# Weight ring buffers of 4128 instead of 4096 bytes a partition in a two-layer attention trunk

## The chip, the cores and the metric

One core of a Trainium2 chip. The metric is the device time of one execution in microseconds; the kernel before takes 651.13 us, the median of three runs (650.99 to 651.28). It must return the reference's output.

## The reference, cut to what matters

x is 256 tokens of 1024 channels, all float32. Each of two layers does this:

```python
h = rms_norm(x, gain)
proj = einsum('bsd,de->bse', h, w_in)              # 1024 -> 9808 columns
(qa, ka, va, ga, qb, kb, vb, gb, qc, kc, vc, gc,
 q_idx, k_idx, w_idx, f_logit, merge_logit) = split(proj)
oa = moba_attention(rope(qa), rope(ka), va) * silu(ga)
ob = dsa_attention(rope(qb), rope(kb), vb, rope(q_idx), rope(k_idx), w_idx) * silu(gb)
oc = forgetting_attention(qc, kc, vc, log_sigmoid(f_logit + f_bias)) * silu(gc)
y = einsum('nbsw,nwd->bsnd', stack([oa, ob, oc]), w_branch)
merged = sum(sigmoid(merge_logit) * y, over n)
x = x + merged @ w_out
```

A last RMS norm follows. The weights (w_in, w_branch, w_out) are read once each, 104 MB in all, and every weight meets all 256 tokens.

## The kernel before, in words

**Precision.** TensorE works on the type float32r. To come near float32, each operand is held as two tiles, a high part (h) and the rest (l), and a product is three matmuls: high times high, low times high, high times low. The normalised and transposed input is hTh and hTl (eight slices of 128 channels by 256 tokens each); the gated branch outputs are og0h, og0l, og1h, og1l; V and, later, the merged sum are in v0 and v1.

**The weights' way.** A chunk of weights, up to 1 MB, comes by a DMA on SP's queue into one of three raw buffers (2048 columns). ScalarE writes the high part of a piece of it (1024 columns) into a buffer wh (L350), VectorE subtracts and writes the rest into wl (L354), both in `piece`. wh and wl are two rings of six buffers each (`R_RING = 6`). `piece` uses the first a * b columns of a buffer and nothing else.

**Units of TensorE.** A projection unit (`unit_b`) takes one pair wh, wl, and writes 128 output columns for all 256 tokens: sixteen matmuls with a slice of wh stationary, for each slice one with hTh and one with hTl moving, then eight with wl stationary and hTh moving, in groups of six (`mm_ops`, L395); a matmul is 128x128 by 256 columns. There are 64 such units in a layer, and one like them whose weights have 80 columns (kwf). A branch unit (`unit_y`) has twelve matmuls: for each of four slices wh with the branch's high and low part, then wl with the high part. There are 24 in a layer, and two of them share a pair wh, wl. In the units for V and for the output (`unit_a`, and `first_v` with L938) the ring buffer is the moving operand of 512 columns and hTh, hTl or V is the stationary one; a unit takes four pairs wh, wl and has 24 matmuls. The last two output units of the kernel are one of 512 columns split in two of 256.

**Between the units** stand the scores of a head pair (`scores`, L558 to L560), transposes of the probabilities (L648) and their product with V (L663 to L666), with VectorE and ScalarE doing the softmax, the rotary embedding, and the choice of keys (L772, L792, L793).

**Order.** `Plan` lists all operations with an estimated cost, a due time, what they read and write and which ring buffer they need, and simulates the engines: at each step it takes, for the engine that is free first, the ready operation with the lowest due time, and emits it. Costs come from functions of the number of columns (t_act, t_dve, t_mm and the like). The order of every engine, the DMAs' order and the turn of the ring buffers are fixed by that when the kernel is built.

**Addresses.** All tiles lie in one pool, each tile behind the one declared before it, in steps of 32 bytes a partition. Starts in a partition, modulo 256: hTh and hTl 192; v0, v1 and the og tiles 0; the block-diagonal keys bd 0; raw0 to raw2 192; wh0 to wh5 and wl0 to wl5 all 192, since 4096 is a multiple of 256; behind the rings q (qh, ql) 192, e 192, pth and ptl 64. A slice of hTh, og or bd lies a multiple of 512 bytes behind its tile's start, and so does a slice of a full weight piece; a slice of the 80-column piece is 320 bytes long, so that its slices start at 192, 0, 64, 128 and so on.

The lines that the change and the prediction touch:

```python
R_RING = 6
tag("raw", R_RAW, [128, 2048])
tag("wh", R_RING, [128, 1024], F32R)
tag("wl", R_RING, [128, 1024], F32R)
p[0].v = T(p[0])[:, :a * b].rearrange("p (a b) -> p a b", a=a)          # L349
ACT.activation(p[0].v, sel(c.v), AF.Copy)                               # L350
DVE.tensor_tensor(p[1].v, sel(c.v), p[0].v.bitcast(F32), op=ALU.subtract)   # L354
his = [(lambda k=k: p[0].v[:, k], lambda k=k, h=h: h[:, k], [p[0]] + hT_all[i])
       for k in range(KC) for i, h in enumerate((hTh, hTl))]            # L412
PE.matmul(o(), a(), b(), start=first and i == 0, stop=last and i == n - 1)  # L395
```

Of the kernel before, what the change touches and what calls it, by code (L numbers as in the profile page):

```python
# [10 lines left out]
F32R = mybir.dt.float32r  # L11
# [20 lines left out]

R_RING = 6
R_RAW = 3
LAG = {("ACT", "DVE"): 142.0, ("DVE", "ACT"): 128.0, ("DVE", "POOL"): 155.0, ("POOL", "ACT"): 75.0,
       ("ACT", "POOL"): 75.0, ("PE", "ACT"): 197.0, ("PE", "DVE"): 196.0, ("PE", "POOL"): 200.0,
       ("ACT", "PE"): 170.0, ("DVE", "PE"): 200.0, ("POOL", "PE"): 170.0,
# [61 lines left out]
class Plan:  # L99
# [37 lines left out]
    def run(self, slack):  # L137
# [4 lines left out]
        while ready:  # L142
            best = {}
            cand = []
            for o in ready:
# [15 lines left out]
                for w in o.ways:  # L161
                    e = w[0]
                    tt = max(t, free.get(e, 0.0))
                    for b in o.bufs:
                        if b.last is not None and b.last.eng != e:
                            tt = max(tt, b.last.end + LAG.get((b.last.eng, e), SEM))
                    for d in o.deps:
                        tt = max(tt, d.end + d.lag + LAG.get((d.eng, e), 0.0 if d.eng == e else SEM) + (0.0 if d.eng == e else o.margin))
                    if e == "POOL" or (e == "DVE" and o.port):
# [64 lines left out]
def hybrid_trunk(ctx, tc, x, norm_gain, w_in, forget_bias, w_branch, w_out, final_gain, consts, out):  # L234
# [9 lines left out]
    def tag(name, n, shape, dt=F32):  # L244
        plan.tag(name, [pool.tile(shape, dt, name=f"{name}{i}") for i in range(n)])
# [67 lines left out]
    k_acc = [Tok() for _ in range(KC)]  # L313

    tag("raw", R_RAW, [128, 2048])
    tag("wh", R_RING, [128, 1024], F32R)
    tag("wl", R_RING, [128, 1024], F32R)
    plan.tag("bd", bd)
    for nm, n, cols, dt in (("qh", 3, S, F32R), ("ql", 3, S, F32R), ("rsh", 2, S, F32), ("rr", 2, S, F32),
                            ("th", 2, S, F32), ("g", 4, S, F32), ("e", 4, 384, F32), ("st", 8, 8, F32),  # L320
# [737 lines left out]
```

## Time and profile before

| | |
|---|---|
| median of three runs | 651.13 us (650.99 to 651.28) |
| the profiled execution | 651.38 us, of which the span shown is 649.5 us |
| TensorE matmuls busy | 639.6 us, 4836 records |
| weight loads busy | 610.9 us |
| VectorE busy | 550.0 us |
| ScalarE busy | 398.8 us |
| DMA, mean | 163 GB/s, 105.56 MB |

The span is the time from the first to the last of the program's own instructions. A TensorE matmul is pipelined: its recorded duration (some 280 ns for 256 columns) is longer than the time from its start to the next one's start, which is what a stream of them costs. The timeline lists starts; a row "x4" stands for four like instructions in a row, and the next row's start is that of the matmul behind them. Times in the timeline have two decimals, so that an interval is best taken over many matmuls and divided.

### The profile page before, as it was taken

How to read it: one execution, taken by the hardware profiler on the slowest of the kernel's cores; microseconds unless marked ns; L12 is line 12 of the kernel's file. 1: busy time of each engine (PE TensorE's matmuls, PEld its weight loads, DVE VectorE, ACT ScalarE, POOL GpSimd, SP SyncE). 2: the span in 40 equal slices, each digit the busy share in tenths (PEclk: the TensorE clock that was granted, in tenths of full speed). 3: DMA queues.
4: the chain of work that ended last, by engine and by line, in shares of the span. 5: the costliest groups of instructions: out<-in, count | busy, mean ns of one | idle time of the engine just before them, and what ended most of it. 6: DMA issues, size and time to landing. Idle time of an engine off the chain costs nothing.

```text
span 649.5 us, 12568 instructions
## 1 busy us (share of the span) xinstructions
PE 639.6 (98%) x4836; PEld 610.9 (94%) x4836; DVE 550.0 (85%) x1334; ACT 398.8 (61%) x799; POOL 89.0 (14%) x96
## 2 busy tenths in 40 slices
PE   8999999999999999999999999999999999999996
PEld 7999999899998999999889999998999989999985
DVE  8899998876969889998488999878587888999873
ACT  6765575764756667575486646767466565747531
POOL 1324112000000222200005403020000003121000
PEclk9999999999999999999999999999999999999998
DMA  9747446455472553473455545634635354453611
GB/s 296 230 143 244 131 130 227 131 166 170 150 229 66 177 173 123 146 256 134 150 175 166 174 143 166 217 97 163 207 118 195 109 178 140 160 162 121 236 34 66
DMA packets 93854, 105.56 MB, mean 163 GB/s; under 512 B 4321, under 2 KB 82401, under 8 KB 93793
## 3 DMA queue, kind: packets, MB, share of 16 engines
q1 hardware_dynamic: 93504, 104.36, 48.7%
q8 instruction: 38, 0.62, 0.4%
q10 hardware_dynamic: 288, 0.39, 0.2%
q14 instruction: 24, 0.19, 0.1%
HBM read 103.69 MB, written 1.05 MB: 161 GB/s over the span
## 4 chain that ended last, share of the span: by engine, by line
PE 83%; DVE 12%; issue 2%; DMA 1%; ACT 1%; SPq 0%; POOL 0%; POOLq 0%; ACTq 0%
PE proj L395 72%; DVE wl L354 4%; PE t L648 2%; PE proj L938 1%; PE s L560 1%; PE s L558 1%; PE o L666 1%; PE s L559 1%; DVE e L621 1%; DMA x<-in_x_dram 1%; PE o L663 1%; DVE isc L793 1%; DVE isc L772 1%; DVE t L792 1%; DVE rsh L440 1%
## 5 line engine op out<-in xcount | busy, mean ns | idle before, releaser
L350 ACT ACTIVATE wh<-raw 128x1024 fp32r<-128x1024 f32 (+1 forms) x190 | 199.5, 1054 | 147.8 <-PE proj L395 125.8
L354 DVE TENSOR_TENSOR wl<-raw,wh 128x1024 fp32r<-128x1024 f32 (+1 forms) x190 | 238.7, 1265 | 41.0 <-ACT wh L350 36.5
L395 PE MATMUL proj<-hTh,wh 128*128 128x256 f32 (+1 forms) x1040 | 257.5, 284 | 0.1
L395 PE MATMUL proj<-hTl,wh 128*128 128x256 f32 (+1 forms) x1040 | 255.9, 283 | 0.0
L395 PEld LDWEIGHTS proj<-hTh,wh 128*128 128x128 f32 (+1 forms) x1040 | 198.2, 191 | 1.6 <-DVE bd1l L697 0.3
L395 PEld LDWEIGHTS proj<-hTl,wh 128*128 128x128 f32 (+1 forms) x1040 | 198.4, 191 | 1.1
L395 PE MATMUL proj<-hTh,wl 128*128 128x256 f32 (+1 forms) x1040 | 149.1, 284 | 0.0
L395 PEld LDWEIGHTS proj<-hTh,wl 128*128 128x128 f32 (+1 forms) x1040 | 135.1, 191 | 0.3
L441 POOL TENSOR_TENSOR rsh<-rsh,cst 128x256 f32<-128x256 f32 (+1 forms) x42 | 35.2, 838 | 419.2 <-DVE rsh L440 419.2
L625 ACT ACTIVATE e<-e,st 128x128 f32<-128x128 f32 x96 | 42.7, 446 | 15.8 <-DVE st L621 15.6
L443 POOL TENSOR_TENSOR rr<-rr,rsh 128x256 f32<-128x256 f32 (+1 forms) x42 | 48.5, 1157 | 10.4 <-DVE rr L442 7.6
L395 PE MATMUL proj<-og0h,wh 128*128 128x256 f32 x128 | 35.7, 279 | 0.0
L395 PE MATMUL proj<-wh,v 128*128 128x512 f32 (+1 forms) x144 | 35.7, 368 | 0.0
L395 PE MATMUL proj<-og0l,wh 128*128 128x256 f32 x128 | 35.6, 278 | 0.0
L395 PE MATMUL proj<-og0h,wl 128*128 128x256 f32 x128 | 35.6, 278 | 0.0
L395 PE MATMUL proj<-wh,hTh 128*128 128x512 f32 x80 | 32.7, 409 | 0.1
L395 PE MATMUL proj<-wh,hTl 128*128 128x512 f32 x80 | 31.4, 393 | 0.0
L395 PEld LDWEIGHTS proj<-wh,v 128*128 128x128 f32 x144 | 25.0, 187 | 5.0
L651 ACT ACTIVATE pth<-t 128x384 fp32r<-128x384 f32 x48 | 22.5, 486 | 9.1 <-PE t L648 9.0
L653 DVE TENSOR_TENSOR ptl<-t,pth 128x384 fp32r<-128x384 f32 x48 | 25.8, 550 | 0.7 <-ACT pth L651 0.5
L395 PE MATMUL proj<-wl,hTh 128*128 128x512 f32 x80 | 24.7, 390 | 0.0
L395 PEld LDWEIGHTS proj<-og0h,wh 128*128 128x128 f32 x128 | 24.0, 188 | 0.2
(190 smaller groups left out, 1026.2 us busy)
## 6 DMA issues: line engine op xcount, KB each, us to landing
raw<-in_w_in_dram SPq DMA_DIRECT2D x74, 1024.0 KB, 5.0
raw<-in_w_branch_dram SPq DMA_DIRECT2D x24, 512.0 KB, 3.4
raw<-in_w_out_dram SPq DMA_DIRECT2D x8, 1024.0 KB, 5.2
raw<-in_w_in_dram SPq DMA_DIRECT2D x3, 512.0 KB, 7.4
x<-in_x_dram SPq DMA_DIRECT2D x4, 256.0 KB, 4.7
raw<-in_w_in_dram SPq DMA_DIRECT2D x2, 320.0 KB, 6.2
out_dram<-tmp SPq DMA_DIRECT2D x2, 320.0 KB, 2.4
raw<-in_w_in_dram SPq DMA_DIRECT2D x2, 256.0 KB, 3.5
```

Of the source, the lines that this page charges most:

```text
L350: ACT.activation(p[0].v, sel(c.v), AF.Copy)
L354: DVE.tensor_tensor(p[1].v, sel(c.v), p[0].v.bitcast(F32), op=ALU.subtract)
L395: PE.matmul(o(), a(), b(), start=first and i == 0, stop=last and i == n - 1)
L440: dve(lambda: DVE.stream_shuffle(T(sh)[:np_], a(), SWAP), S, [ps], [sh], key, "rope")
L441: gps(lambda: POOL.tensor_tensor(T(sh)[:np_], T(sh)[:np_], s[:np_], op=ALU.mult), S, [k_rope], [sh], key, "rope")
L443: gps(lambda: POOL.tensor_tensor(T(r)[:np_], T(r)[:np_], T(sh)[:np_], op=ALU.add), S, [sh], [r], key, "rope")
L558: PE.matmul(o, qh[:, sl], kh[:, :, :n], start=True, stop=False)
L559: PE.matmul(o, ql[:, sl], kh[:, :, :n], start=False, stop=False)
L625: act(lambda t=t, a=a, n=n, e=e, st=st: ACT.activation(T(e)[:, a:a + n], T(e)[:, a:a + n], AF.Exp, bias=T(st)[:, t:t + 1], scale=-1.0, acc ...
L648: PE.transpose(T(ps)[:, i * 128:(i + 1) * 128], T(es[h])[:, i * 128:(i + 1) * 128], ident)
L651: act(lambda h=h, src=src: ACT.activation(T(ph)[:, h], src(), AF.Copy), 384, True, [ps], [kp[h][0]], key, "pT", touch=[ph])
L653: dve(lambda h=h, src=src: DVE.tensor_tensor(T(pl)[:, h], src(), T(ph)[:, h].bitcast(F32), op=ALU.subtract), 384, [ps, kp[h][0]], [kp[h][1 ...
```

## The change

Each ring buffer gets eight float32 columns, 32 bytes, that nothing writes or reads.

```diff
 R_RING = 6
 R_RAW = 3
+STAGGER = 8
...
     tag("raw", R_RAW, [128, 2048])
-    tag("wh", R_RING, [128, 1024], F32R)
-    tag("wl", R_RING, [128, 1024], F32R)
+    tag("wh", R_RING, [128, 1024 + STAGGER], F32R)
+    tag("wl", R_RING, [128, 1024 + STAGGER], F32R)
```

The twelve buffers then start, modulo 256, at 192, 224, 0, 32, 64, 96 (wh0 to wh5) and 128, 160, 192, 224, 0, 32 (wl0 to wl5). Everything declared behind them moves by 12 x 32 = 384 bytes: q and e to 64, pth and ptl to 192. The tiles ahead of them (hTh, hTl, v, og, bd, raw) stay. The pool ends 384 bytes higher, at 229,056 bytes of a partition.

## Rows read from the trace of the kernel before

**Rows 1.** The page: the span, and busy time by engine.

```profile
span 649.5 us, 12568 instructions
PE 639.6 (98%) x4836; PEld 610.9 (94%) x4836; DVE 550.0 (85%) x1334; ACT 398.8 (61%) x799; POOL 89.0 (14%) x96
```

**Rows 2.** Busy time of each engine by stretches, with granted clock and DMA.

```profile
core 0: us, PE busy (x) PEld busy (x) DVE busy (x) ACT busy (x) POOL busy (x), PEclk, DMA share, GB/s
...
25.00:90.00 65.00, 64.72 (x521) 63.24 (x520) 63.54 (x182) 38.72 (x72) 22.26 (x22) 1.00 0.49 160
...
130.00:215.00 85.00, 84.87 (x651) 81.02 (x651) 66.92 (x154) 52.86 (x106) 0.00 (x0) 1.00 0.48 154
...
345.00:415.00 70.00, 70.00 (x565) 68.64 (x566) 66.63 (x188) 44.79 (x87) 21.20 (x22) 1.00 0.46 151
```

**Rows 3.** The page: the chain that ended last, by engine and by line.

```profile
PE 83%; DVE 12%; issue 2%; DMA 1%; ACT 1%; SPq 0%; POOL 0%; POOLq 0%; ACTq 0%
PE proj L395 72%; DVE wl L354 4%; PE t L648 2%; PE proj L938 1%; PE s L560 1%; PE s L558 1%; PE o L666 1%; PE s L559 1%; DVE e L621 1%; DMA x<-in_x_dram 1%; PE o L663 1%; DVE isc L793 1%; DVE isc L772 1%; DVE t L792 1%; DVE rsh L440 1%
```

**Rows 4.** Groups of instructions by shape, whole span: projection matmuls (count, busy us, mean ns).

```profile
L395 PE MATMUL proj<-hTh,wh 128*128 128x256 f32 x1024 | 253.7, 284 | 0.1
...
L395 PE MATMUL proj<-hTh,wl 128*128 128x256 f32 x1024 | 146.9, 284 | 0.0
```

**Rows 5.** Timeline of TensorE, a projection unit (start us, us, instruction): sixteen matmuls apart.

```profile
145.10 0.28 PE L395 MATMUL proj<-hTh,wh 128*128 128x256 f32 x1
...
147.02 0.64 PE L395 MATMUL proj<-hTh,wl 128*128 128x256 f32 x4
```

**Rows 6.** Timeline, two branch units (24 matmuls), and the projection unit behind them.

```profile
139.39 0.28 PE L395 MATMUL proj<-og0h,wh 128*128 128x256 f32 x1
...
142.22 0.29 PE L395 MATMUL proj<-hTh,wh 128*128 128x256 f32 x1
142.35 0.28 PE L395 MATMUL proj<-hTl,wh 128*128 128x256 f32 x1
142.46 0.29 PE L395 MATMUL proj<-hTh,wh 128*128 128x256 f32 x1
...
142.82 0.28 PE L395 MATMUL proj<-hTl,wh 128*128 128x256 f32 x1
```

**Rows 7.** Timeline, another branch unit, behind a block of scores: eighteen matmuls apart.

```profile
160.98 0.28 PE L395 MATMUL proj<-og0h,wh 128*128 128x256 f32 x1
...
163.02 0.28 PE L395 MATMUL proj<-og0h,wh 128*128 128x256 f32 x1
```

**Rows 8.** Timeline, units of 512 columns: six matmuls apart, then twelve apart.

```profile
207.67 0.39 PE L395 MATMUL proj<-wh,hTh 128*128 128x512 f32 x1
...
209.03 0.39 PE L395 MATMUL proj<-wh,hTh 128*128 128x512 f32 x1
...
304.49 1.09 PE L395 MATMUL proj<-wh,v 128*128 128x512 f32 x4
...
307.29 1.09 PE L395 MATMUL proj<-wh,v 128*128 128x512 f32 x4
```

**Rows 9.** Timeline, the 80-column unit: its first matmul and the next unit's, 24 apart.

```profile
22.47 0.28 PE L395 MATMUL proj<-hTh,wh 128*80 128x256 f32 x1
...
25.28 0.28 PE L395 MATMUL proj<-hTh,wh 128*128 128x256 f32 x1
```

**Rows 10.** Groups by shape, whole span: the weight splits, and two operations of 256 columns.

```profile
L354 DVE TENSOR_TENSOR wl<-raw,wh 128x1024 fp32r<-128x1024 f32 x188 | 237.1, 1270 | 41.0 <-ACT wh L350 36.5 <-PE proj L395 2.0 <-ACT og1h L385 1.2
L350 ACT ACTIVATE wh<-raw 128x1024 fp32r<-128x1024 f32 x188 | 198.1, 1058 | 147.8 <-PE proj L395 125.8 <-issue 9.1 <-DMA raw<-in_w_in_dram 7.9
...
L684 DVE TENSOR_TENSOR ot<-ot,g 128x256 f32<-128x256 f32 x24 | 10.0, 418 | 0.3
L386 DVE SCALAR_TENSOR_TENSOR og0l<-ot,og0h 128x256 fp32r<-128x256 f32 x16 | 6.7, 418 | 0.0
```

**Rows 11.** Groups by shape from 25 to 90 us, then from 345 to 415 us: projection matmuls.

```profile
L395 PE MATMUL proj<-hTh,wh 128*128 128x256 f32 x155 | 38.3, 283 | 0.0
...
L395 PE MATMUL proj<-hTh,wh 128*128 128x256 f32 x168 | 41.6, 284 | 0.0
```

## The prediction

> **What bounds the kernel now.** I read the share of busy time first, then the stages, the chain, and last the timeline of TensorE. The page gives TensorE 639.6 of 649.5 us and VectorE 550.0 [rows 1]. By stages TensorE is full, and VectorE is full beside it in two stretches, 25 to 90 us (63.5 of 65.0) and 345 to 415 us (66.6 of 70.0); at 130 to 215 us it has 18 us to spare [rows 2]. The chain that ended last is 83% TensorE and 12% VectorE, and 72% of the span is one line, the matmuls of L395 [rows 3]. The granted clock is 1.00 in these stretches, so the 2.4 GHz level [rows 2]. So what counts is the time from one matmul's start to the next. The mean duration of 284 ns in the groups [rows 4] is not that: matmuls overlap. It has to be read from start times.
>
> 256 columns at 2.4 GHz are 106.7 ns. In a projection unit with hTh or hTl moving and a ring buffer stationary, sixteen starts lie in 1.92 us, 120.0 ns each [rows 5]. In a branch unit (og moving, ring stationary, same shape) 24 lie in 2.83 us, 117.9 ns [rows 6]; in another branch unit 18 lie in 2.04 us, 113.3 ns [rows 7]. With 512 columns and the ring moving, six take 1.36 us (226.7 ns) with hTh stationary, and twelve take 2.80 us (233.3 ns) with V stationary [rows 8]. Same engine, clock and shape, but steady values that differ by up to 6%, and which value goes with which pair of tiles. The starts of the tiles modulo 256 differ between these pairs: hTh, hTl and all ring buffers at 192, og and V at 0. My theory: while a matmul streams its moving operand, the next weight load reads too, and what they cost each other depends on the two addresses modulo 256. The pair with equal residues has the highest of the steady values for 256 columns.
>
> **The change, part by part.** Instructions, order, waits and DMAs stay: the planner sees neither sizes nor addresses, and raw, the DMAs' target, lies ahead of the ring. What moves is the address of each ring buffer, and of every tile behind the ring, by 384 bytes.
>
> *Projection units* (128 of 24 matmuls, 3072 in all, in three groups of 1024, two of which stand in [rows 4]; the two 80-column units apart). After the change the buffers' residues are 192, 224, 0, 32, 64, 96 for wh and 128, 160, 192, 224, 0, 32 for wl. Sixteen matmuls of a unit use wh, eight wl, each with one of six buffers: 1/6 of them keep the equal residues and 5/6 get another distance, which I take to stay at 120.0 or to go to one of the lower values. Bounds: 120.0 (nothing gained) and 113.3 ns [rows 7], 6.7 ns less. Between them lie 117.9 [rows 6] and the one unit whose stationary pieces already start at changing residues, the 80-column one: 24 matmuls in 2.81 us, 117.1 ns [rows 9]. That is the nearest row, since after the change distances also change from unit to unit; its weight load is shorter, which is the doubt. So 2.9 ns less on 5/6, 2.4 ns on the mean.
>
> Not all of it reaches the end. From 25 to 90 us VectorE is the late one, and there are three groups of about 155 such matmuls [rows 11], 465: I count nothing. From 345 to 415 us (three of 168, 504) VectorE has 3.4 us of slack; I count half. That leaves 3072 - 465 - 252 = 2355 matmuls: 2355 x 2.4 ns = 5.7 us gained. At the bound of 113.3 it is 2355 x 5/6 x 6.7 = 13.1 us, at the other nothing. What is late next is VectorE's split of the weights.
>
> *Branch units* (48 of 12 matmuls, 576): they have 113.3 or 117.9 today and will have six distances, among them zero. Nothing in sum; bounds 576 x 4.6 ns = 2.6 us either way.
>
> *512 columns* (48 of the first unit, 240 more of V, 168 of the output): today 226.7 to 233.3 and will be spread over the same values. Nothing; bounds 456 x 6.7 ns = 3.0 us either way.
>
> *Attention* (q, e and the probabilities lie behind the ring, and go from 192 to 64 and from 64 to 192): 1% to 2% of the span on the chain per line [rows 3]; I count nothing, and 0.5 us either way.
>
> *Switches.* A unit now changes its distance when it goes from wh to wl, and again into the next unit. The trace has such a change: from a branch unit to a projection unit the first five starts take 0.60 us, 120.0 ns each, in steps of 0.13 and 0.11 [rows 6]. No cost on the mean, and a single step of at most 0.13 against 0.12, or 8 ns with rounding allowed for.
>
> *The splits.* ScalarE writes wh, VectorE reads raw and wh and writes wl, 1058 and 1270 ns a piece [rows 10]. VectorE's 128x256 operations take 418 ns with operands at 192 and 192 (ot, g) and with 192 and 0 (ot, og0h) [rows 10]: no sign of the address. For steps of 32 bytes there is no row. Nothing; bound: 1% of 190 splits is 2.4 us, of which the 25 to 90 us stretch, the only one that VectorE sets, would show a tenth or so.
>
> Sum: 5.7 us off. The profiled execution took 651.38 us (span 649.5), the median is 651.13: 645.7 and 645.4. I say 645.5.
>
> The Trainium skill speaks against all of this: "SBUF — State Buffer", section "Who interferes with whom", says that TensorE and ScalarE never wait on anyone, and "TensorE: Matmul & The Clock Gate", section "Step-by-step: what each phase is for", that loading the next weights does not steal read bandwidth from the running matmul. By these the sum would be zero and the time 651.1; the trace does not agree that the interval is one number per shape (113.3, 117.9 and 120.0 ns), though it does not show the cause.
>
> **The rivals.** The bound in which a measurement of this kernel can tell a change from none is about 0.2%, 1.3 us.
>
> *No effect.* The interval could hang on the sequence of instructions (pairs wh, wh against wh, wh, wl; 80 columns) and not on addresses; then 651.1. For it: one and the same pairing, og with the ring, has both 117.9 and 113.3, so history matters. Against it: the value is steady over whole units and over both layers, and projection units come back to 120.0 from any start.
>
> *Deep gain.* Most distances settle at 113.3, as the branch unit behind a score block did [rows 7]. 13.1 us, plus up to 2.6 of the branch units: 651.1 - 13.1 - 1.5 = 636.5. For it: two of the pairings seen hold their lowest value (113.3 [rows 7], 226.7 [rows 8]) as a steady state. Against it: VectorE's second full stretch would take the gain there.
>
> *Slower, by switches.* Steady values do not fall, and each change of distance costs the 8 ns of the largest single step [rows 6]. The kernel would then have 2 x 128 in projection units, 2 for each of 192 triples in branch units, and 8 in each of 19 units of 512 columns or their halves: 256 + 384 + 152 = 792 switches, 6.3 us, 657.4. It decides when a switch costs more than the gain, 5.7 us / 792 = 7 ns. Against it: the five starts behind the switch that the trace has come to 120.0. For it: residues at odd multiples of 32, which half the buffers get, occur nowhere in the trace for a large tile, and may be a worse case than any seen.
>
> That the change doesn't do what it says is true in part: with steps of 32 bytes modulo 256 there are eight places, so wl2 to wl5 lie where wh0 to wh3 do. What matters for the theory is the distance to the other operand, which is zero for two of twelve.
>
> **How the numbers follow.** Forecast (1.3 to 9 us faster) 0.48; deep gain 0.20; no effect 0.14; slower 0.18. So faster 0.68, same 0.14, slower 0.18. The range reaches from the deep gain with all bounds on its side but a part (634) to half the price of the switches (654); beyond each end I leave about 0.06. The likeliest case alone is 642 to 650.
>
> **What would show it.** In the timeline of the changed kernel, projection units with wh0 would stay at 120.0 ns a start, and others show 113 to 118; the mean of the groups in [rows 4] would fall by 2 to 3 ns. VectorE's 25 to 90 us stretch would stay as long as it is. The duration of the splits [rows 10] would stay. I am wrong if all units stay at 120.0 (no effect), if units at odd multiples of 32 show more than 120.0, or if TensorE's intervals fall and the span does not, VectorE taking all of it.

## The result, and the profile after

The changed kernel takes 647.46 us, the median of five runs (646.85 to 648.84), against 651.13 us. The ratio is 0.9949, with an interval of 0.9935 to 0.9964: faster by 3.7 us, or 0.5%. The lines shown of a kernel come from one execution, which can be slower than its median (by 2.6 us at most, with hT at 128).

The profiled execution took 647.42 us. The page gives its span, the busy time by engine, and the chain that ended last; these lines answer to [rows 1] and [rows 3].

```profile
span 645.6 us, 12568 instructions
PE 634.3 (98%) x4836; PEld 605.0 (94%) x4836; DVE 549.9 (85%) x1334; ACT 398.5 (62%) x799; POOL 89.1 (14%) x96
...
PE 86%; DVE 9%; issue 1%; DMA 1%; ACT 1%; SPq 0%; POOL 0%; POOLq 0%; ACTq 0%
```

The same instructions, as many on each engine, and only TensorE and its weight loads have a different busy time: 639.6 to 634.3 us. VectorE and ScalarE are where they were. TensorE gave up 5.3 us and the span 3.9, so 1.4 us of it came back as idle time of TensorE; the stretches below show where. The chain does not show it: VectorE's share of it fell, from 12% to 9%.

The groups by shape show which matmuls gave it. These answer to [rows 4] and [rows 10]; all line numbers are one higher than before.

```profile
L396 PE MATMUL proj<-hTh,wh 128*128 128x256 f32 x1024 | 250.1, 282 | 0.0
L396 PE MATMUL proj<-hTl,wh 128*128 128x256 f32 x1024 | 248.2, 281 | 0.0
L355 DVE TENSOR_TENSOR wl<-raw,wh 128x1024 fp32r<-128x1024 f32 x188 | 237.5, 1272 | 38.9 <-ACT wh L351 36.2 <-ACT og1h L386 1.2 <-PE proj L396 0.7
L351 ACT ACTIVATE wh<-raw 128x1024 fp32r<-128x1024 f32 x188 | 198.3, 1059 | 142.2 <-PE proj L396 122.4 <-issue 8.8 <-DMA raw<-in_w_in_dram 8.3
...
L396 PE MATMUL proj<-hTh,wl 128*128 128x256 f32 x1024 | 144.1, 281 | 0.0
...
L396 PE MATMUL proj<-og0h,wh 128*128 128x256 f32 x128 | 35.9, 281 | 0.0
L396 PE MATMUL proj<-og0h,wl 128*128 128x256 f32 x128 | 35.8, 280 | 0.0
...
L396 PE MATMUL proj<-wl,hTh 128*128 128x512 f32 x80 | 25.1, 394 | 0.0
```

The means of the projection groups fell by 2 to 3 ns (284 to 282 and 281). The splits stayed at 1272 and 1059 ns. Two kinds went the other way; in the kernel before, the same view has:

```profile
L395 PE MATMUL proj<-hTl,wh 128*128 128x256 f32 x1024 | 252.1, 283 | 0.0
...
L395 PEld LDWEIGHTS proj<-hTl,wh 128*128 128x128 f32 x1024 | 196.0, 191 | 0.9
...
L395 PE MATMUL proj<-og0h,wh 128*128 128x256 f32 x128 | 35.7, 279 | 0.0
...
L395 PE MATMUL proj<-og0h,wl 128*128 128x256 f32 x128 | 35.6, 278 | 0.0
...
L395 PE MATMUL proj<-wh,v 128*128 128x512 f32 x112 | 30.7, 395 | 0.0
L395 PE MATMUL proj<-wl,hTh 128*128 128x512 f32 x80 | 24.7, 390 | 0.0
```

Branch matmuls went from 279 and 278 to 281 and 280 ns, the 512-column ones with hTh stationary from 390 to 394. A mean duration is about 164 ns longer than the interval for 256 columns (284 beside 120.0, [rows 4, 5]), so differences between means read as differences between intervals.

The timeline of TensorE shows it unit by unit. Three projection units of the changed kernel, first with wh0 (192 modulo 256, where hT is), then wh1 (224), then wh2 (0); the sixteen matmuls with wh end where the line with wl begins:

```profile
147.62 0.29 PE L396 MATMUL proj<-hTh,wh 128*128 128x256 f32 x1
147.75 0.28 PE L396 MATMUL proj<-hTl,wh 128*128 128x256 f32 x1
...
149.54 1.07 PE L396 MATMUL proj<-hTh,wl 128*128 128x256 f32 x8
150.45 0.28 PE L396 MATMUL proj<-hTh,wh 128*128 128x256 f32 x1
...
152.34 1.09 PE L396 MATMUL proj<-hTh,wl 128*128 128x256 f32 x8
153.27 0.28 PE L396 MATMUL proj<-hTh,wh 128*128 128x256 f32 x1
...
155.09 1.00 PE L396 MATMUL proj<-hTh,wl 128*128 128x256 f32 x7
```

Sixteen starts take 1.92, 1.89 and 1.82 us: 120.0, 118.1 and 113.8 ns each. These units differ in the address of the stationary operand, and in what runs ahead of them.

Last, where in the span the time came off. The first matmul of a block of scores is a mark that both runs have; for each tile the view of its line gives the first and the last start (us), here of the whole span and of three stretches. Before:

```profile
L558 PE MATMUL s<-bd0h,qh x24: 278/376/397, 36.6 to 587.7; 128*128 128x256 f32 x12, 128*128 128x512 f32 x12
...
L558 PE MATMUL s<-bd0h,qh x2: 283/340/397, 114.6 to 115.0; 128*128 128x256 f32 x1, 128*128 128x512 f32 x1
...
L558 PE MATMUL s<-bd1h,qh x8: 282/380/397, 354.2 to 368.6; 128*128 128x256 f32 x4, 128*128 128x512 f32 x4
...
L558 PE MATMUL s<-bd0h,qh x2: 365/381/397, 403.9 to 404.4; 128*128 128x256 f32 x1, 128*128 128x512 f32 x1
```

And after:

```profile
L559 PE MATMUL s<-bd0h,qh x24: 277/378/398, 36.8 to 583.9; 128*128 128x256 f32 x12, 128*128 128x512 f32 x12
...
L559 PE MATMUL s<-bd0h,qh x2: 277/335/393, 114.5 to 114.8; 128*128 128x256 f32 x1, 128*128 128x512 f32 x1
...
L559 PE MATMUL s<-bd1h,qh x8: 280/376/398, 352.2 to 366.4; 128*128 128x256 f32 x4, 128*128 128x512 f32 x4
...
L559 PE MATMUL s<-bd0h,qh x2: 363/380/398, 401.8 to 402.2; 128*128 128x256 f32 x1, 128*128 128x512 f32 x1
```

At 115 us the changed kernel is 0.1 us ahead (0.2 behind at 37 us); at 354 us 2.0, at 404 us 2.1, at 588 us 3.8. Next to nothing was gained up to 115 us, or between 354 and 404 us. The busy times of these stretches say why (they answer to [rows 2]):

```profile
25.00:90.00 65.00, 64.09 (x521) 62.30 (x520) 63.32 (x179) 38.80 (x71) 22.31 (x22) 1.00 0.50 160
...
130.00:215.00 85.00, 84.99 (x658) 81.08 (x657) 67.59 (x155) 53.25 (x108) 0.00 (x0) 1.00 0.48 158
...
345.00:415.00 70.00, 69.35 (x572) 67.97 (x572) 67.02 (x185) 44.79 (x87) 20.04 (x20) 1.00 0.48 155
```

From 25 to 90 us TensorE does the same 521 matmuls in 64.09 in place of 64.72 us of busy time, and waits for the difference, 0.91 us in place of 0.28: VectorE is full. From 345 to 415 us it waits 0.65 us in place of none. Where VectorE has room, as from 130 to 215 us, TensorE stays full and does 658 matmuls in place of 651.

### The profile page after: what moved, and what is told of

Read it like the earlier page. It is cut to its first block, busy times and chain, and to the rows that moved or that the text cites. A ratio compares the mean times of both kernels' runs of the same rounds, so it can differ in the third digit from the quotient of the medians.

```text
span 645.6 us, 12568 instructions
## 1 busy us (share of the span) xinstructions
PE 634.3 (98%) x4836; PEld 605.0 (94%) x4836; DVE 549.9 (85%) x1334; ACT 398.5 (62%) x799; POOL 89.1 (14%) x96
## 4 chain that ended last, share of the span: by engine, by line
PE 86%; DVE 9%; issue 1%; DMA 1%; ACT 1%; SPq 0%; POOL 0%; POOLq 0%; ACTq 0%
PE proj L396 74%; DVE wl L355 3%; PE t L649 2%; PE s L561 1%; PE proj L939 1%; PE s L559 1%; PE s L560 1%; PE o L667 1%; DMA x<-in_x_dram 1%; PE o L664 1%; DVE isc L794 1%; DVE isc L773 1%; DVE t L793 1%; DVE rsh L441 1%; PE t L604 1%
## 5 line engine op out<-in xcount | busy, mean ns | idle before, releaser
L396 PE MATMUL proj<-hTh,wh 128*128 128x256 f32 (+1 forms) x1040 | 253.9, 282 | 0.0
L396 PE MATMUL proj<-hTl,wh 128*128 128x256 f32 (+1 forms) x1040 | 252.1, 281 | 0.0
L396 PEld LDWEIGHTS proj<-hTh,wh 128*128 128x128 f32 (+1 forms) x1040 | 195.6, 188 | 1.5 <-DVE bd1l L698 0.2
L396 PEld LDWEIGHTS proj<-hTl,wh 128*128 128x128 f32 (+1 forms) x1040 | 195.5, 188 | 1.2
L396 PE MATMUL proj<-hTh,wl 128*128 128x256 f32 (+1 forms) x1040 | 146.3, 281 | 0.0
L396 PEld LDWEIGHTS proj<-hTh,wl 128*128 128x128 f32 (+1 forms) x1040 | 132.3, 188 | 0.3
L396 PEld LDWEIGHTS proj<-og0l,wh 128*128 128x128 f32 x128 | 24.2, 189 | 0.2
```

## The experiments

The theory: the interval of a stream of matmuls hangs on the distance modulo 256 between the moving operand and the ring buffer or tile that is loaded meanwhile, and equal residues are a bad case. Rivals: that the variety of addresses helps, not the distance; that the place of the ring itself counts; that the gain came with the attention tiles that moved too. The medians of the kernel before beside these runs were 651.13, 651.42 and 650.84 us. For each run I worked out the mean interval from the starts of all matmuls that follow each other in the trace, steps over 1.2 times the columns at 2.4 GHz plus 20 ns left out (some 3030 of 3072 projection pairs are left); the means of the groups beside them say the same more coarsely. In the kernel before they are 119.8 ns for projection units, 116.9 for branch units, 229.8 for 512 columns with hT stationary and 233.4 with V. The trace leaves buffer numbers out; which buffer a unit has follows from the order of the matmuls in the kernel.

### The whole ring at one other address

```diff
     tag("raw", R_RAW, [128, 2048])
+    pool.tile([128, 16], F32, name="padf")
     tag("wh", R_RING, [128, 1024], F32R)
     tag("wl", R_RING, [128, 1024], F32R)
+    pool.tile([128, 48], F32, name="padb")
```

All twelve buffers move by 64 bytes, from 192 to 0, and what lies behind them by 256, so to the same residues. The distance of hT to the ring goes from 0 to 192.

> All twelve ring buffers, 4096 bytes long as before, start at 0 modulo 256 (64 bytes left free ahead of the rings, 192 behind, so that everything behind them keeps its residue). Theory 'distance': the interval of two matmuls is set by the distance of moving and stationary operand modulo 256. Projection units (hTh at 192, ring at 0) go from 119.8 to about 114.9 ns, the value that such pairs have in the changed kernel; the mean duration of their groups falls from 284 to about 278-279 ns. Branch units get distance zero and go up to about 120 (duration 283). In sum 8 to 12 us less than before: 639 to 643 us. Rival 'variety': the change gained because distances change all the time and no steady state at 120 can form; then one distance for all gives a steady state as before, and 651 us within 1.3. Rival 'no cause in addresses': 651.

Measured: 638.17 us (637.79 to 639.85), ratio 0.9802 [0.9785, 0.982], a little below the range. Busy time on the page, and a row by stretches:

```profile
PE 624.2 (98%) x4836; PEld 595.4 (93%) x4836; DVE 548.4 (86%) x1334; ACT 398.3 (62%) x799; POOL 89.0 (14%) x96
...
345.00:415.00 70.00, 68.64 (x578) 66.91 (x578) 67.71 (x187) 44.55 (x87) 17.43 (x18) 1.00 0.49 161
```

TensorE's busy time falls by 15.4 us, and the span of this execution by 11.5. Part of what TensorE saves is idle time now: from 345 to 415 us, with VectorE nearly full, it waits 1.36 us, where it waited for nothing before. The chain is no measure of this: VectorE has 17% of it here, and 12% in the second execution of the same kernel, further down. The groups by shape:

```profile
L397 PE MATMUL proj<-hTh,wh 128*128 128x256 f32 x1024 | 242.6, 278 | 0.1
...
L397 PE MATMUL proj<-og0h,wh 128*128 128x256 f32 x128 | 36.2, 283 | 0.0
...
L397 PE MATMUL proj<-wh,v 128*128 128x512 f32 x112 | 30.1, 390 | 0.0
```

The projection group falls from 284 to 278 (113.9 ns a start), and the kernel gains 13.0 us, three and a half times what the change did. So it is not variety: all buffers lie at one residue again, only another one. The branch units, where og now has the residue of the ring, rise from 279 to 283 (119.6 ns): the bad case has moved to them. V with 512 columns falls from 395 to 390 (227.1 ns), though its distance goes from 192 to 0: with 512 columns the distances rank another way. With hT stationary, 192 has 233.5 ns (the next run) and 0 has 229.8.

The opposite place, 192 bytes ahead and 64 behind, puts the ring at 128:

```diff
+    pool.tile([128, 48], F32, name="padf")
     tag("wh", R_RING, [128, 1024], F32R)
     tag("wl", R_RING, [128, 1024], F32R)
+    pool.tile([128, 16], F32, name="padb")
```

> All ring buffers start at 128 modulo 256 (192 bytes free ahead, 64 behind). Theory 'distance': projection units 114 to 115 ns (as pairs at this distance in the changed kernel, 114.9), durations of their groups 278-279 ns, branch units about 117, so 639 to 643 us. Rival 'variety': 651. If the two kernels with one residue differ by more than 3 us, the branch and the 512-column units make the difference.

Measured: 647.59 us (647.49 to 649.23), ratio 0.9948 [0.9931, 0.9965]. Two of its groups by shape:

```profile
L397 PE MATMUL proj<-hTh,wh 128*128 128x256 f32 x1024 | 249.5, 281 | 0.0
...
L397 PE MATMUL proj<-hTh,wl 128*128 128x256 f32 x1024 | 144.6, 280 | 0.0
```

This one missed the 639 to 643 us and the 114 to 115 ns that I expected: 281 and 280, 117.7 ns a start. I had taken that figure from the changed kernel's pairs with a buffer at 128, whose mean is 114.9. In a stretch of this distance alone the interval is another; the run with wl at 128, below, takes that up.

### Controls: the same distances at other places

256 bytes ahead of the ring move ring and all behind it by a whole period:

```diff
+    pool.tile([128, 64], F32, name="padf")
     tag("wh", R_RING, [128, 1024], F32R)
     tag("wl", R_RING, [128, 1024], F32R)
```

> Control: 256 bytes free ahead of the rings, so that every ring buffer and every tile behind moves, and no residue modulo 256 changes. Theory 'distance': 651.1 within 0.5 us, groups of projection matmuls at 284 ns as before. Rival 'position': what counts is where the buffers lie, not modulo 256; then the time moves by more than 1.3 us.

Measured: 651.11 us (650.61 to 653.11), ratio 0.9995 [0.9983, 1.0007], groups at 284, 283 and 284 as before. Where the ring lies counts modulo 256 only, or not at all.

384 bytes behind the ring and none ahead of it move the attention tiles as the change does, and the ring not:

```diff
     tag("wh", R_RING, [128, 1024], F32R)
     tag("wl", R_RING, [128, 1024], F32R)
+    pool.tile([128, 96], F32, name="padb")
```

> The rings as before (all at 192), 384 bytes free behind them, so that the tiles behind the rings move as in the change. This is the attention's part of the change alone. Theory: within 0.5 us of 651.1, groups of projection matmuls at 284 ns. Rival: the tiles behind the rings make the gain; then 647.5.

Measured: 650.97 us (650.36 to 654.27), ratio 0.9998 [0.9984, 1.0013]. The move of q, e and the probabilities is worth nothing.

64 bytes ahead of all tiles give every tile another residue and leave every distance:

```diff
+    pool.tile([128, 16], F32, name="pad0")
     cst = pool.tile([128, C_END], F32, name="cst")
```

> 64 bytes ahead of everything: every tile moves from its place by 64 bytes, all distances stay. Distance theory: no change, groups of the projection units at 284, branch units near 279, 651.1 +- 0.7 us. Rival (places modulo 256 by themselves count): projection groups at 278 to 282, and a time below 649 us.

Measured: 651.08 us (650.63 to 654.82), ratio 1.0001 [0.9984, 1.0017]. Projection groups at 284, 283 and 284, the branch groups at 279 and 278: the ring is at 0 here, the place that gained 13 us in the first experiment, and it gains nothing when hT goes along. So the place by itself is out.

### The distance made from the other side

The ring stays at 192, and hTh and hTl go to 128:

```diff
+    pool.tile([128, 48], F32, name="padh")
     hTh = pool.tile([128, KC, S], F32R, name="hTh")
     hTl = pool.tile([128, KC, S], F32R, name="hTl")
+    pool.tile([128, 16], F32, name="padk")
```

> The kernel before with hTh and hTl moved from 192 to 128 (modulo 256); the ring stays at 192, og and V at 0, so that only the distance of hT minus ring changes, from 0 to 192. Distance theory: as with the ring at 0, where the same distance was made by moving the ring: projection units at 113.9 ns a start (groups near 278 ns), branch units as before (groups near 279), the span 10 to 13 us shorter, 638 to 641 us. Rival (the place of the ring buffer by itself sets the interval, 192 being a bad one): projection units stay at 120.0 ns (284), 651.1 +- 0.7 us.

Measured: 639.14 us (639.01 to 641.76), ratio 0.9823 [0.9803, 0.9844]. Its groups by shape:

```profile
L397 PE MATMUL proj<-hTh,wh 128*128 128x256 f32 x1024 | 245.0, 280 | 0.2
L397 PE MATMUL proj<-hTl,wh 128*128 128x256 f32 x1024 | 243.2, 278 | 0.0
...
L397 PE MATMUL proj<-og0h,wh 128*128 128x256 f32 x128 | 35.7, 279 | 0.0
```

The time came out as expected, by moving the other operand. The intervals are 115.2 ns, a little above the 113.9 forecast. This mean is a mixture. Two units of the same trace, with one and the same distance, the second of them behind a block of scores:

```profile
232.41 0.28 PE L397 MATMUL proj<-hTh,wh 128*128 128x256 f32 x1
...
234.22 1.07 PE L397 MATMUL proj<-hTh,wl 128*128 128x256 f32 x8
...
236.18 0.28 PE L397 MATMUL proj<-hTh,wh 128*128 128x256 f32 x1
...
238.06 1.10 PE L397 MATMUL proj<-hTh,wl 128*128 128x256 f32 x8
```

Sixteen starts take 1.81 us (113.1 ns each) and 1.88 us (117.5). Taking the last six intervals with wh in each of the 128 units, 78 units end near 113.5 ns and 50 near 117.7; with the ring at 0 it is 116 and 12, and 105 and 23 when that kernel ran again. So the distance 192 takes the units off 120 ns, and a unit then holds one of two lower intervals. Together with the controls this shows the distance as the cause of leaving 120 ns; which of the two lower ones a unit holds it does not settle.

### A distance that is an odd multiple of 32

The whole ring at 96, with 160 bytes ahead and 96 behind:

```diff
+    pool.tile([128, 40], F32, name="padf")
     tag("wh", R_RING, [128, 1024], F32R)
     tag("wl", R_RING, [128, 1024], F32R)
+    pool.tile([128, 24], F32, name="padb")
```

> All twelve ring buffers at 96 (modulo 256), so that hT minus ring is 96, an odd multiple of 32, and V and og minus ring 160. Theory that each distance has its own value: pairs of this distance had the highest mean of the changed kernel's eight (119.9 ns), so projection units at 118 to 121 ns (groups 282 to 285) and 649 to 653 us. Rival (any distance but zero gains): projection units at 114 to 118 ns (groups 278 to 282), 638 to 648 us.

Measured: 653.69 us (652.38 to 654.39), ratio 1.0032 [1.0019, 1.0045]: slower than before, and 0.7 us above the range. Its groups by shape:

```profile
L397 PE MATMUL proj<-hTh,wh 128*128 128x256 f32 x1024 | 253.7, 284 | 0.0
L397 PE MATMUL proj<-hTl,wh 128*128 128x256 f32 x1024 | 251.9, 281 | 0.0
...
L397 PEld LDWEIGHTS proj<-hTl,wh 128*128 128x128 f32 x1024 | 193.0, 188 | 1.0
...
L397 PE MATMUL proj<-og0h,wh 128*128 128x256 f32 x128 | 36.0, 281 | 0.0
...
L397 PE MATMUL proj<-wl,hTh 128*128 128x512 f32 x80 | 25.1, 395 | 0.0
```

The projection units stay at 119.8 ns: 96 is as bad a distance as 0, so "any distance but zero" is out. What makes the kernel slower is, by the intervals, the rest: branch units 118.5 for 116.9 ns (570 pairs, 0.9 us), 512 columns with hT stationary 233.8 for 229.8 (288, 1.2 us), the last 48 of 256 columns with V 120.0 for 113.6 (0.3 us). That sums to 2.4 us, beside 2.3 measured (0.2% to 0.4%); no run took these terms apart.

### Does an interval carry over?

wh at 0 and wl at 128, so that the distance 64 stands behind sixteen matmuls of distance 192:

```diff
+    pool.tile([128, 16], F32, name="padf")
     tag("wh", R_RING, [128, 1024], F32R)
+    pool.tile([128, 32], F32, name="padm")
     tag("wl", R_RING, [128, 1024], F32R)
+    pool.tile([128, 16], F32, name="padb")
```

> The six wh buffers at 0 and the six wl buffers at 128 (modulo 256): hT minus ring is 192 for the sixteen matmuls with wh and 64 for the eight with wl. With the whole ring at 128 the distance 64 settled at 117.7 ns; in the changed kernel, where it stands between others, its pairs had a mean of 114.9. Theory A (a low interval, once reached, is carried over into the pairs of distance 64): the group of wl stays at 277 to 279, near 114 to 115 ns, and the time at 638 to 639.5 us. Theory B (each distance has one value of its own): the group of wl at 280 to 281, 117.7 ns, the groups of wh at 277 to 278; 1024 x 3.8 ns = 3.9 us more than with the whole ring at 0, of which 3 to 3.9 in the span, 641 to 642 us.

Measured: 639.54 us (638.79 to 640.7), ratio 0.9824 [0.9809, 0.9839]. Its groups by shape:

```profile
L398 PE MATMUL proj<-hTh,wh 128*128 128x256 f32 x1024 | 243.2, 279 | 0.2
L398 PE MATMUL proj<-hTl,wh 128*128 128x256 f32 x1024 | 241.3, 277 | 0.0
L398 PE MATMUL proj<-hTh,wl 128*128 128x256 f32 x1024 | 141.3, 278 | 0.0
```

The group of wl is at 278, and its some 1000 pairs have 114.3 ns, where the same distance alone had 117.7. That is theory A: a low interval is carried into a distance that by itself settled higher. The higher one is carried too: in all 21 units whose wh part ends near 117.7 ns, the wl part ends there as well. And in none of the traces with the distance 192 or 64 does a stretch of these matmuls, as long as no other matmul and no wait breaks it, go from the lower interval to the higher one (counted in groups of six intervals: 1708 follow a low group, and all 1708 are low). After a break it begins on the higher one in 23 of 62 stretches here, and with the whole ring at 128 in 61 of 62.

The time lies a little above A's range and 1.2 us above the ring at 0 (638.31 us in the run below), but the intervals of the two ratios overlap. V with 512 columns is at 231.1 ns here in place of 227.1, 0.7 us on 168 matmuls; the projection units have 114.3 ns in both traces. The rest stays open.

### The branch units too

The ring at 0 and the og tiles at 192, so that both moving operands have the distance 192:

```diff
+    pool.tile([128, 48], F32, name="pado")
     og = [[pool.tile([128, 4, S], F32R, name=f"og{i}{p}") for p in "hl"] for i in range(2)]
+    pool.tile([128, 16], F32, name="padq")
...
     tag("raw", R_RAW, [128, 2048])
+    pool.tile([128, 16], F32, name="padf")
     tag("wh", R_RING, [128, 1024], F32R)
     tag("wl", R_RING, [128, 1024], F32R)
+    pool.tile([128, 48], F32, name="padb")
```

> Ring at 0 as in the first experiment, and the og tiles moved to 192 as well, so that og minus ring is 192 in place of 0. Distance theory: projection units as there (groups near 278, 113.9 ns), branch units fall from 119.6 ns to about 113.5 (groups from 283 to about 277): 570 x 6.1 ns = 3.5 us on TensorE, of which 2 to 3.5 in the span, 634.7 to 636.2 us. Rival (VectorE is the late one by now, or the branch units hold their value by the order of their matmuls): 637.5 to 638.5 us.

Measured: 637.5 us (636.58 to 638.48), ratio 0.9786 [0.977, 0.9803]. The branch units did fall, to 277 (114.3 ns), but the time lay on the rival's side, with runs (636.58 to 638.48) in the rival's range and between the two: not clear. So this kernel and that of the first experiment ran again, side by side and with more runs. The ring alone at 0:

> The first experiment's kernel once more, with more runs, beside the next one on the same chip: 637.8 to 639 us, groups of the projection units at 277 to 278, of the branch units at 283.

Measured: 638.31 us (637.97 to 639.92), ratio 0.9807 [0.9791, 0.9823]. And with og:

> The kernel with the ring at 0 and og at 192 once more, with more runs. Its branch units take 114.3 ns in place of 119.6 with the ring alone at 0: 570 x 5.3 ns = 3.0 us on TensorE. If half or more of it reaches the end: 1.5 to 3 us below the kernel beside it, 635.5 to 637 us. If VectorE's splits take it: less than 1 us below it, 637.2 to 638.2 us.

Measured: 636.57 us (636.37 to 637.47), ratio 0.9779 [0.9766, 0.9793]. Busy time on the page:

```profile
PE 621.5 (98%) x4836; PEld 592.9 (93%) x4836; DVE 548.1 (86%) x1334; ACT 398.5 (63%) x799; POOL 89.1 (14%) x96
```

And of its groups by shape:

```profile
L399 PE MATMUL proj<-og0h,wh 128*128 128x256 f32 x128 | 35.5, 277 | 0.0
```

1.7 us below the kernel beside it, over half of the 3.0 us on TensorE: this is the fastest kernel of the study, 14.3 us under the kernel before, by 512 bytes of padding a partition. The medians of both pairs agree on the sign; their intervals overlap a little, so the size of this last step is less sure.

## Why the prediction was right

The time came as forecast in sign and nearly in size: 3.7 us in place of 5.6, by the mechanism of the prediction, which lacks one thing: a distance can hold two intervals. By its steps:

- **Projection units**: forecast 2.4 ns on the mean (5/6 of the pairs, 2.9 ns each), measured 2.2 (119.84 to 117.68). The pairs at 120.0 and others near the bound of 113.3 both occur, as the three units above show. Two distances of the eight kept 119.8, 0 and 96, with 809 of 2978 pairs in place of the sixth that the prediction left there; the others lie 3.0 ns lower on the mean. On 3072 matmuls it is 6.6 us of TensorE's time.
- **What doesn't reach the end**: forecast nothing of the 25 to 90 us stretch and half of the 345 to 415 us one. Measured: 0.1 us up to 115 us, and 0.1 between 354 and 404 us, where half would be some 0.4. The waits were where the prediction put them, and the second took more than half; on the 2355 matmuls that it counted, 2.2 ns make 5.1 us.
- **Branch units and 512 columns**, forecast to give nothing in sum, are the mis-sized terms. Branch units went from 116.9 to 117.7 ns (570 pairs, 0.5 us), 512 columns with hT stationary from 229.8 to 232.4 (288, 0.7 us); V with 512 columns fell from 233.4 to 232.0 (168, 0.2 us), and the last 48 of 256 columns rose from 113.6 to 118.6 (0.2 us). Together 1.2 us lost. With it the sum is 5.1 - 1.2 = 3.9 us, which is what the span shows. That they meet to the tenth is luck in part: the half of 345 to 415 us did not come, and not all of the 1.2 us need be lost where TensorE is late. The prediction had their bounds (2.6 and 3.0 us), but took the middle, where these pairs, but for V with 512 columns, stood nearer their good values before. That the branch units lost by being spread is not shown: they went to 117.6 ns also with 384 bytes behind the ring and with hT at 128, where og kept its distance of 64.
- **Attention**: nothing, as forecast; shown, as a time, by the control with 384 bytes behind the ring.
- **Switches**: the first step into the unit with wh0 is 0.13 us, the 0.13 of the forecast, and the unit's sixteen still take 1.92 us. No cost on the mean.
- **The splits**: 1272 and 1059 ns, as before.
- **The rivals**: no effect fell with the first runs, though its remark that history matters holds (two intervals at one distance). The deep gain did not come from the change, but the ring at one good residue came close to its size (13.0 us against 14.6 worked out). The slower end fell with the price of the switches; its remark that odd multiples of 32 may be worse than any seen is half right: 96 is as bad as 0, no worse, while in the changed kernel pairs with a buffer at 32 (distance 160) have 117.8 ns and those at 224 (distance 224) 118.1.

On the two pages that spoke against the change: a sum by them would have given 651.1. That TensorE never waits on anyone (the Trainium skill, "SBUF — State Buffer", section "Who interferes with whom") no run here contradicts as far as other engines go, since the two operands are TensorE's own. But the Trainium skill, "TensorE: Matmul & The Clock Gate", section "Step-by-step: what each phase is for", also has the loading of the next weights not steal read bandwidth from the running matmul; the same 3072 matmuls take 119.8 ns each or 113.9 to 115.2, by the distance of the two operands alone (0 and 192), so for this shape the time of the two together is not free of their addresses.

What goes on inside the chip is not shown: which two reads meet, and why 64 bytes more or less part them, no row says. Nor was a rule for all eight distances sought: with hT moving, 32, 128, 160 and 224 were seen only in the mixture of the changed kernel. Nor is it shown what settles, at a break in the stream, which of the two lower intervals comes next.

## What to carry to other kernels

Where TensorE is full and like matmuls settle at different steady intervals, compare the start addresses modulo 256 of the moving tile and of the tile that is loaded as weights, and try one of them moved by a few dozen bytes: moving the ring by 64 bytes was worth 2% here, while a different address for every buffer averaged good and bad distances and got 0.5%. Equal residues were the bad case with 256 columns only; with 512, V had 227.1 ns at distance 0 and 233.4 at 192, so no distance is good for all shapes. Read the interval from start times, for each pair of tiles and unit by unit, since a mean can mix two steady values, and look at what the move does to the other pairs. A gain on TensorE counts only in the stretches where no other engine is as full.

## What the runs showed of the hardware that was not expected

The granted clock was the same in the stretches compared (1.00, the 2.4 GHz level), and yet 256 columns have three steady intervals, near 113.5, 117.7 and 120 ns, and 512 columns have 226.7 to 233.8. One and the same distance can hold two of them: 64 settles at 117.7 ns by itself and at 114.3 behind pairs of distance 192, and 192 has units at both 113.5 and 117.7. The lower of the two, once reached, lasted until the stream was broken. The distances 0 and 96 stayed near 120.

The weight loads show something of their own: with equal residues they take 191 ns (before, above), and 188 at a distance of 96, though the interval is 120 ns in both. So the longer load is not what sets the interval.
